# A hybrid encoder block on one core: the second half of the attention values and the first head pair as one operand of 512 columns, and the memory attention started behind later token blocks

## The chip, the core and the metric

The kernel runs on one core of a Trainium2 chip. A core has a matrix engine (TensorE, PE in the profile, with its weight loads as PEld), three elementwise engines (VectorE or DVE, ScalarE or ACT, GpSimd or POOL), a queue that issues transfers (SyncE or SP), an on-chip memory of 128 partitions, and a small accumulator memory of eight banks into which TensorE writes. The metric is the device time of one execution in microseconds; lower is better.

## The reference

One layer of a hybrid encoder on x (1024 tokens x 1024 channels) and a memory of 256 tokens. After an RMS norm, one input projection gives the inputs of three mixers and three sigmoid gates:

```python
h = _rmsnorm(x, norm_mix_g[l])
z = h @ w_in[l]
(hq, hf, hi, hg, fq, fk, fv, ff, mq, gate_logits) = split(z)
y_a = _hgrn2_mixer(hq, hf, hi, hg, ...)              # gated linear recurrence, 4 heads
y_b = _fox_mixer(fq, fk, fv, ff, fox_f_bias, ...)    # forgetting attention, 8 heads of 64
mem_kv = _rmsnorm(mem, norm_mem_g[l]) @ mem_kv_w[l]
y_c = _memory_mixer(mq, mem_kv, ...)                 # cross-attention into 256 memory tokens, 4 heads of 128
gates = sigmoid(gate_logits).reshape(B, T, 3, D_MODEL)
merged = gates[:, :, 0] * (y_a @ w_br_hgrn) + gates[:, :, 1] * (y_b @ w_br_fox) + gates[:, :, 2] * (y_c @ w_br_mem)
x = x + merged @ w_out
x = x + _conv_glu_ffn(_rmsnorm(x, norm_ffn_g[l]), ffn_w_up, ffn_conv_w, ffn_conv_b, ffn_w_down)
```

The forgetting attention needs, for each token, 512 values (fv), 8 forget logits (ff), and queries and keys of 8 heads (fq, fk). The memory attention normalizes its queries per head (a sum of squares over 128 channels), takes their products with 256 memory keys as logits, a softmax, and the product with the memory values.

## The kernel before

All matmuls are done on operands split into a rounded high part and a low remainder; a product is three matmuls (high x high, high x low, low x high) issued by `mm3` (lines 246 to 250). A split is a cast on ScalarE (line 254, the helper of all casts) and a subtraction on VectorE (line 262).

The program runs in stages. A dense stage computes most gates and the memory queries with a fast block scheme (`dense_unit`, products of the families T1 to T4, until about 267 us in the trace). Then comes the stage of this study:

- `token_major` (line 793) computes a projection with tokens on partitions. For each of 8 blocks of 128 tokens it issues 8 x 3 matmuls into one accumulator bank: the token block of `uh`/`ul` is the stationary operand, the split weights `wh`/`wl` are the moving one with `ncol` columns. An `evac` function then scales the bank by the tokens' norm and copies it out on ScalarE.
- `fox_values` (line 824) calls it twice: values 0 to 255 into `Vf` (256 columns, line 827), then values 256 to 511 with the 8 forget logits (264 columns, lines 827 and 829). After the second it turns the forget logits into cumulative log decays: absolute value, sigmoid and logarithm on ScalarE (lines 833 to 835), 8 transposes on TensorE (line 840), two scans on VectorE (line 841), and a store to DRAM.
- `fox_proj` (line 967) computes keys and queries of head pair 0 (256 columns) into `z` (line 973) and normalizes them in halves of four blocks (lines 979 to 982).
- `memory` (line 924) is the memory attention. `mem_prep(h)` loads the queries of a head (`mqf`, line 868), squares them (line 873), sums the squares with 8 one-column matmuls (line 876), and splits them into `mqh`/`mql`. `mem_parts` loads the memory's keys and values (`mkv`, line 858) and splits them. `mem_attn(h)` does, for each half of the tokens, logits (`mm3` into `lg`), maximum (897), exponential (901), normalization on GpSimd (905), transposes (912), a split, the product with the values (`po`), and a split and two stores of the result.

`weave` (line 98) traces these generators alternately: at each turn the one that is least far through its stated number of steps advances. The token work counts 25 steps, the memory 28, and both begin at share 0. The memory's instructions are traced under a priority 300 places ahead (`ahead`, line 236). The order on each engine within the stage is then made by a scheduler that puts together priority and expected readiness. The transfers are issued on SP in order.

Weights go through `weights` (line 276): a raw buffer (two in all, 512 KB a load), and a slot of a ring of four pairs `wh`/`wl` (`WIDE`), taken in turn. A piece of 1,024 columns holds four of the eight channel chunks of a 256-column projection, or two of a 512-column one.

After the weave come the weights of head pair 1 (`parts[-1]`, line 1332) and a stage whose order on every engine is written by a planner (`Plan`): first the tokens of pair 1 (line 1229, 256 columns), the transposes of `z` (line 1038), and then the forgetting attention.

Of the kernel before, what the change touches and what calls it, by code (L numbers as in the profile page):

```python
# [9 lines left out]
F32R = mybir.dt.float32r  # L10
AF = mybir.ActivationFunctionType
ALU = mybir.AluOpType
# [25 lines left out]

HGRN_STEPS, MEM_STEPS = 14, 7
AHEAD = 300  # L40
SLACK = 0.8
WIDE = 4
SEQ = ("w0 x0 s0 w1 x1 s1 w2 x2 s2 w3 x3 s3 w4 x4 s4 x5 s5 x6 s6 x7 s7 u0 u1 u2 u3 mn u4 u5 u6 u7 lk k0 k1 k2 k3 lx "
# [154 lines left out]
def tile_block(ctx: ExitStack, tc: tile.TileContext, xT, memT, x_rows, mem_rows, vec, fbias, mats, hmask, w_first, w_cm, w_late, w_fqk, w_fv,  # L198
# [47 lines left out]
    def mm3(ps, lh, ll, rh, rl, first, last, more=False):  # L246

        PE.matmul(ps, lh, rh, start=first, stop=False, skip_group_check=more)  # L248
        PE.matmul(ps, lh, rl, start=False, stop=False, skip_group_check=more)  # L249
        return PE.matmul(ps, ll, rh, start=False, stop=last, skip_group_check=more)  # L250
# [542 lines left out]
    def token_major(src, ncol, evac, lead=False):  # L793

        with tc.issue_after(late["load"].ins):
            per = 2 if ncol == HB else 4
            w = [weights(src[q], (per, ncol)) for q in range(KC // per)]
        if lead:
            yield
        for tb in range(8):  # L800
            ps = ps_proj()[:, :ncol]
            tsl = slice(tb * P, (tb + 1) * P)
            for k in range(KC):
                wh, wl = w[k // per]
                mm3(ps, uh[k][:, tsl], ul[k][:, tsl], wh[:, k % per, :], wl[:, k % per, :], k == 0, k == KC - 1)
            evac(tb, ps)
            yield


# [12 lines left out]
    negFd = tc.dram_tile([8, T], F32, name="negFd")  # L822

    def fox_values():
        for pc in range(2):
            def evac(tb, ps, pc=pc):
                S.activation(Vf[:, tb, pc * 256:(pc + 1) * 256], ps[:, :256], AF.Copy, scale=rt[:, tb:tb + 1])
                if pc:
                    V.scalar_tensor_tensor(out=ffx[:, tb, :], in0=ps[:, 256:264], scalar=rt[:, tb:tb + 1], in1=fbr,
                                           op0=ALU.mult, op1=ALU.add)  # L830
            yield from token_major(w_fv[pc], 264 if pc else 256, evac)

        S.activation(ffe, ffx, AF.Abs)
        S.activation(ffe, ffe, AF.Sigmoid)
        S.activation(ffe, ffe, AF.Ln)
# [27 lines left out]
    def mem_prep(h):  # L863
        mqh = pm.tile([P, T], F32R, tag="mqh", name=f"mqh_{h}", bufs=2)
        mql = pm.tile([P, T], F32R, tag="mql", name=f"mql_{h}", bufs=2)
        rq = pm.tile([P, 8], F32, tag="rq", name=f"rq_{h}", bufs=2)
        t = pm.tile([P, T], F32, tag="mqf", name=f"mqf_{h}", bufs=2)
        SP.dma_start(t, mqd[h])
        prs = ps_tr()
        for n in range(2):  # L870
            sl = slice(n * HB, (n + 1) * HB)
            sq = pm.tile([P, HB], F32, tag="msq2", name="msq2")
            S.activation(sq, t[:, sl], AF.Square)
            for b in range(4):
                tb = 4 * n + b
                PE.matmul(prs[:, tb:tb + 1], sq[:, b * P:(b + 1) * P], ones[:, 0:1], start=True, stop=True)
        split(S, mqh, mql, t)
        V.tensor_mul(rq, prs[:, :8], rt)
        V.tensor_mul(rq, rq, rt)
        rstd_small(rq, rq, P)  # L880
        V.tensor_mul(rq, rq, rt)
        mset[h] = (mqh, mql, rq)
        yield

    def mem_attn(h):
        mqh, mql, rq = mset[h]
        for n in range(2):
            pts = []
            for j in range(2):
                ps = ps_lg()  # L890
                pt = pm.tile([P, 2, NM], F32, tag="mpt", name="mpt", bufs=3)
                st = pm.tile([P, 8], F32, tag="mst", name="mst", bufs=3)
                tb = 4 * n + 2 * j
                for b in range(2):
                    tsl = slice((tb + b) * P, (tb + b + 1) * P)
                    mm3(ps[:, b * NM:(b + 1) * NM], mqh[:, tsl], mql[:, tsl], mkh[:, h, :], mkl[:, h, :], True, True)
                V.reduce_max(st[:, 0:2], ps.rearrange("p (b m) -> p b m", b=2), axis=AX.X)
                V.scalar_tensor_tensor(out=st[:, 2:4], in0=st[:, 0:2], scalar=-1.0, in1=rq[:, tb:tb + 2],
                                       op0=ALU.mult, op1=ALU.mult)
                for b in range(2):  # L900
                    S.activation(pt[:, b, :], ps[:, b * NM:(b + 1) * NM], AF.Exp, bias=st[:, 2 + b:3 + b],
                                 scale=rq[:, tb + b:tb + b + 1], accum_out=st[:, 4 + b:5 + b])
                V.reciprocal(st[:, 6:8], st[:, 4:6])
                for b in range(2):
                    G.tensor_scalar(pt[:, b, :], pt[:, b, :], st[:, 6 + b:7 + b], 0.0, ALU.mult, ALU.add)
                pts.append(pt)
                yield
            po = ps_po()
            for m in range(2):
                ptr = ps_tr()  # L910
                for b in range(4):
                    PE.transpose(ptr[:, b * P:(b + 1) * P], pts[b // 2][:, b % 2, m * P:(m + 1) * P], ident)
                ph = pm.tile([P, HB], F32R, tag="mph", name="mph", bufs=2)
                pl = pm.tile([P, HB], F32R, tag="mpl", name="mpl", bufs=2)
                split(S, ph, pl, ptr)
                hv = slice(h * P, (h + 1) * P)
                mm3(po, mvh[:, m, hv], mvl[:, m, hv], ph, pl, m == 0, m == 1)
            yt = [pm.tile([P, HB], F32R, tag=t, name=t, bufs=2) for t in ("ych", "ycl")]
            split(S, *yt, po)
            for t, d in zip(yt, ycd):  # L920
                SP.dma_start(d[:, h, n * HB:(n + 1) * HB], t.bitcast(F32))
            yield

    def memory():
        run_all(mem_prep(0))
        mem_parts()
        yield
        for h in range(4):
            if h < 3:
                run_all(mem_prep(h + 1))  # L930
            yield from mem_attn(h)
# [35 lines left out]
    def fox_proj():  # L967

        def evac(tb, ps):
            n, b = tb // 4, tb % 4  # L970
            if b == 0:
                fox_tile(0, n)
            S.activation(fox_z[0, n][:, b, :], ps, AF.Copy, scale=rt[:, tb:tb + 1])
            if b == 3:
                z = fox_z[0, n].rearrange("p b (h d) -> p (b h) d", d=64)
                r = cp.tile([P, 16], F32, tag="fr", name="fr", bufs=2)
                for i in range(2):
                    sq = gate_tile().rearrange("p (h d) -> p h d", d=64)
                    S.activation(sq, z[:, 8 * i:8 * i + 8, :], AF.Square)
                    V.reduce_sum(r[:, 8 * i:8 * i + 8], sq, axis=AX.X)  # L980
                rstd_small(r, r, 64)
                V.tensor_mul(z, z, r.unsqueeze(2).to_broadcast([P, 16, 64]))

        yield from token_major(w_fqk[0], 256, evac)

    qk, qk_ready, vh, vh_ready, nfs, nf_ready = {}, {}, {}, {}, {}, {}
    pt_ready, pt_free, rows_done, turn, kept = {}, {}, {-1: 0.0, -2: 0.0}, {}, {}
# [1108 lines left out]
def _layout(inp):  # L2096
# [6 lines left out]
    def kmaj(a):  # L2103

        return a.reshape(a.shape[0] // P, P, a.shape[1]).transpose(1, 0, 2)
# [52 lines left out]
    def pieces(a, cuts):  # L2158
        out = []
        for lo, hi_ in cuts:  # L2160
# [1 line left out]
            out.append(np.stack([p[:, 0:4].reshape(P, -1), p[:, 4:8].reshape(P, -1)]))  # L2162
        return out

    o["w_fqk"] = c(np.stack([pieces(np.concatenate([fk[:, p * P:(p + 1) * P], fq[:, p * P:(p + 1) * P]], axis=1),
                                    [(0, 256)])[0] for p in range(2)]))
    late = np.concatenate([m[:, p * P:(p + 1) * P] for p in (2, 3) for m in (fk, fq)], axis=1)
    o["w_late"] = c(np.stack([kmaj(m).reshape(P, 4, 2 * HB).transpose(1, 0, 2) for m in (late, hi)]))
    pv = pieces(np.concatenate([fv, ff], axis=1), [(0, 256), (256, 520)])
    o["w_fv0"], o["w_fv1"] = c(pv[0]), c(pv[1])  # L2170
# [32 lines left out]
```

## Time and profile before

| what | us |
| --- | --- |
| median of the three runs shown (1689.5 to 1692.33) | 1689.61 |
| the profiled execution's own time | 1688.31 |
| its span in the profile | 1686.5 |
| TensorE busy in the span | 1677.7 |
| VectorE, ScalarE, GpSimd busy | 1170.4, 808.5, 326.6 |
| the stage of this study, from and to | 258, 371 |

The span runs from the first to the last instruction; the execution's own time has the start and the end around it. A busy time of TensorE is made with modelled ends, so that the time of a matmul overlaps the next; what a matmul costs in a row of matmuls is the distance between two starts. Instructions stand under their source line, their output and their inputs (`pp<-wh,uh` is a matmul into a bank of the projections with moving `wh` and stationary `uh`). A time behind an arrow is idle time of the engine and what ended it.

### The profile page before, as it was taken

What the parts mean: (1) busy time and instruction counts of PE and PEld (TensorE: products, weight loads), DVE (VectorE), ACT (ScalarE), POOL (GpSimd) and SP (SyncE); (2) the same over time, 40 slices, a digit from 0 to 9 for tenths busy, and PEclk for the clock granted to TensorE, in tenths of its full rate; (3) what the DMA queues carried; (4) which work ended last, traced back from release to release, by engine and by line L of the source; (5) the groups of instructions that cost most, each with busy time, mean ns of one, the idle gap of its engine ahead of it and who ended that gap; (6) DMA issues with size and microseconds to landing.
All of it is one profiled execution on the core that took longest, in us unless ns stands there. A gap on an engine that the chain in (4) does not pass through costs nothing.

```text
span 1686.5 us, 23254 instructions
## 1 busy us (share of the span) xinstructions
PE 1677.7 (99%) x8409; PEld 1415.8 (84%) x8409; DVE 1170.4 (69%) x2118; ACT 808.5 (48%) x1459; POOL 326.6 (19%) x430
## 2 busy tenths in 40 slices
PE   9999999999999999999999999999999999999999
PEld 7888889998888888888888888888888888888887
DVE  6966554558688766766856745988788888775664
ACT  6734444656576556666521333634344444533432
POOL 0200001336464423433201000211111111100000
PEclk9999999999999999999999999999999999999999
DMA  9442324122142233100337641666454454494782
GB/s 376 171 145 105 118 77 157 71 100 69 57 133 87 75 101 101 51 20 19 107 106 257 207 151 58 189 180 182 132 144 131 122 166 132 176 352 154 239 283 88
DMA packets 87348, 235.50 MB, mean 140 GB/s; under 512 B 9904, under 2 KB 12600, under 8 KB 87104
## 3 DMA queue, kind: packets, MB, share of 16 engines
q1 hardware_dynamic: 68032, 166.83, 28.4%
q0 software_dynamic: 18624, 66.59, 13.9%
q8 instruction: 66, 1.08, 0.3%
q10 hardware_dynamic: 576, 0.59, 0.1%
q14 instruction: 50, 0.41, 0.1%
HBM read 184.91 MB, written 72.13 MB: 152 GB/s over the span
## 4 chain that ended last, share of the span: by engine, by line
PE 96%; DVE 2%; ACT 1%; DMA 1%; issue 0%; ACTq 0%; DVEq 0%
PE pp L250 17%; PE pp L249 17%; PE pp L248 17%; PE pp L1229 10%; PE lg L248 5%; PE lg L250 5%; PE lg L249 5%; PE tr L250 3%; PE tr L249 3%; PE tr L248 3%; PE tr L1147 2%; PE po L1172 1%; PE lg L1085 1%; PE lg L1086 1%; PE po L248 1%; PE po L249 1%
## 5 line engine op out<-in xcount | busy, mean ns | idle before, releaser
L254 ACT CAST wh<-s 128x512 fp32r<-128x512 f32 x122 | 73.3, 620 | 133.1 <-PE pp L249 73.3
L254 ACT CAST wh<-rw 128x512 fp32r<-128x512 f32 x96 | 58.5, 619 | 113.8 <-PE pp L249 69.7
L254 ACT CAST wh<-raw 128x512 fp32r<-128x512 f32 (+2 forms) x85 | 63.9, 756 | 96.0 <-PE pp L249 76.3
L254 ACT CAST dwh<-wr 128x1024 fp32r<-128x1024 f32 (+1 forms) x41 | 40.2, 980 | 114.1 <-PE tr L249 37.6
L250 PE MATMUL pp<-uh,wl 128*128 128x512 f32 x224 | 89.0, 397 | 0.0
L248 PE MATMUL pp<-uh,wh 128*128 128x512 f32 x224 | 88.8, 396 | 0.0
L249 PE MATMUL pp<-ul,wh 128*128 128x512 f32 x224 | 88.4, 395 | 0.0
L1161 DVE TENSOR_TENSOR pl<-tr,ph 128x512 fp32r<-128x512 f32 (+1 forms) x96 | 51.4, 551 | 30.7 <-ACT ph L254 30.3
L1120 ACT ACTIVATE pt<-pt,st 128x128 f32<-128x128 f32 (+3 forms) x64 | 49.6, 775 | 45.9 <-DVE st L1116 30.6
L1229 PE MATMUL pp<-wl,uh 128*128 128x512 f32 (+1 forms) x192 | 70.0, 365 | 0.0
L1229 PE MATMUL pp<-wh,uh 128*128 128x512 f32 (+1 forms) x192 | 69.5, 362 | 0.0
L1229 PE MATMUL pp<-wh,ul 128*128 128x512 f32 (+1 forms) x192 | 69.4, 362 | 0.0
L262 DVE TENSOR_TENSOR dwl<-wr,dwh 128x1024 fp32r<-128x1024 f32 (+1 forms) x41 | 46.3, 1130 | 30.5 <-ACT dwh L254 30.5
L254 ACT CAST ph<-tr 128x512 fp32r<-128x512 f32 (+1 forms) x96 | 44.2, 477 | 41.0 <-PE tr L1147 39.6
L1124 POOL TENSOR_SCALAR pt<-pt,st 128x128 f32<-128x128 f32 (+3 forms) x64 | 52.0, 815 | 60.1 <-DVE st L1122 58.4
L1828 POOL DMA_DIRECT2D rw<-in_w_up x42 | 23.2, 558 | 200.0 <-DVE wl L1718 190.1
L1718 DVE TENSOR_TENSOR wl<-rw,wh 128x512 fp32r<-128x512 f32 x69 | 46.6, 687 | 21.2 <-PE pp L250 17.9
L1718 DVE TENSOR_TENSOR wl<-s,wh 128x512 fp32r<-128x512 f32 x85 | 57.9, 683 | 0.0
L262 DVE TENSOR_TENSOR wl<-raw,wh 128x512 fp32r<-128x512 f32 (+2 forms) x54 | 52.1, 964 | 7.0 <-ACT wh L254 7.0
L248 PE MATMUL pp<-wh,uh 128*128 128x256 f32 (+1 forms) x192 | 55.2, 287 | 0.0
L250 PE MATMUL pp<-wh,ul 128*128 128x256 f32 (+1 forms) x192 | 55.0, 286 | 0.0
L249 PE MATMUL pp<-wl,uh 128*128 128x256 f32 (+1 forms) x192 | 54.4, 283 | 0.0
(520 smaller groups left out, 5602.2 us busy)
## 6 DMA issues: line engine op xcount, KB each, us to landing
rw<-in_w_up POOLq DMA_DIRECT2D x42, 512.0 KB, 4.8
sd<-in_w_dn POOLq DMA_DIRECT2D x30, 512.0 KB, 6.0
br<-yd SPq DMA_DIRECT2D x30, 512.0 KB, 5.6
gd<-gt SPq DMA_DIRECT2D x48, 256.0 KB, 2.0
gt<-gd SPq DMA_DIRECT2D x48, 256.0 KB, 2.8
yd<-fc SPq DMA_DIRECT2D x44, 256.0 KB, 2.8
wr<-sd SPq DMA_DIRECT2D x20, 512.0 KB, 4.9
raw<-in_w_cm SPq DMA_DIRECT2D x18, 512.0 KB, 3.5
```

The costliest lines, as they stand in the source:

```text
L248: PE.matmul(ps, lh, rh, start=first, stop=False, skip_group_check=more)
L249: PE.matmul(ps, lh, rl, start=False, stop=False, skip_group_check=more)
L250: return PE.matmul(ps, ll, rh, start=False, stop=last, skip_group_check=more)
L254: return S.copy(out, in_)
L262: return (sub or V).tensor_sub(l, src, h.bitcast(F32))
L1120: S.activation(pt, pt, AF.Exp, bias=st[:, 2:3], accum_out=st[:, 3:4])
L1124: G.tensor_scalar(pt, pt, st[:, 3:4], 0.0, ALU.mult, ALU.add)
L1147: PE.transpose(ptr[:, j * P:(j + 1) * P], pts[j][:, sb * P:(sb + 1) * P], ident)
L1161: V.tensor_sub(pl[:, c], ptr[:, c], ph[:, c].bitcast(F32))
L1229: PE.matmul(o, a, b, start=q == i == 0, stop=q == KC - 1 and i == 2)
L1718: late["split"] = V.tensor_sub(l, src, h.bitcast(F32))
L1828: late["raw"] = (SP if begun else G).dma_start(raw[:, 2 * i:2 * i + 2, :], src[:, 2 * i:2 * i + 2, :])
```

## The change

The second half of the values and head pair 0 become one operand of 512 columns (`wide`, `w_fv[1]`), computed in one `token_major` pass by `fox_proj`, which evacuates each block twice: 256 columns to `z`, 256 to `Vf`. The first pass now holds the first half of the values with the forget logits (264 columns), so the decays are computed between the two passes. The 512-column weights have four pieces of two chunks; the third one is split into a pair of tiles of its own (`xwh`, `xwl`, from the stage's pool), and the fourth takes the next slot of the ring. The token work counts 17 steps in the weave, and the memory begins at share 0.2 and waits until five token blocks have been traced. For head 0, the matmuls of the norm sums and of the logits are ordered behind the last token matmul traced before them.

```diff
+MEM_START = 0.2
...
         with tc.issue_after(late["load"].ins):
             per = 2 if ncol == HB else 4
-            w = [weights(src[q], (per, ncol)) for q in range(KC // per)]
+            own = [pm.tile([P, 4 * 264], F32R, tag=t, name=t) for t in ("xwh", "xwl")] if ncol == HB else None
+            w = [weights(src[q], (per, ncol), hl=own if q == 2 else None) for q in range(KC // per)]
...
-                mm3(ps, uh[k][:, tsl], ul[k][:, tsl], wh[:, k % per, :], wl[:, k % per, :], k == 0, k == KC - 1)
+                late["tokens"] = mm3(ps, uh[k][:, tsl], ul[k][:, tsl], wh[:, k % per, :], wl[:, k % per, :], k == 0, k == KC - 1)
             evac(tb, ps)
+            late["blocks"] = late.get("blocks", 0) + 1
             yield
...
     def fox_values():
-        for pc in range(2):
-            def evac(tb, ps, pc=pc):
-                S.activation(Vf[:, tb, pc * 256:(pc + 1) * 256], ps[:, :256], AF.Copy, scale=rt[:, tb:tb + 1])
-                if pc:
-                    V.scalar_tensor_tensor(out=ffx[:, tb, :], in0=ps[:, 256:264], scalar=rt[:, tb:tb + 1], in1=fbr,
-                                           op0=ALU.mult, op1=ALU.add)
-            yield from token_major(w_fv[pc], 264 if pc else 256, evac)
+        def evac(tb, ps):
+            S.activation(Vf[:, tb, :256], ps[:, :256], AF.Copy, scale=rt[:, tb:tb + 1])
+            V.scalar_tensor_tensor(out=ffx[:, tb, :], in0=ps[:, 256:264], scalar=rt[:, tb:tb + 1], in1=fbr,
+                                   op0=ALU.mult, op1=ALU.add)
+        yield from token_major(w_fv[0], 264, evac)
...
-                PE.matmul(prs[:, tb:tb + 1], sq[:, b * P:(b + 1) * P], ones[:, 0:1], start=True, stop=True)
+                with tc.issue_after(late["tokens"].ins) if h == 0 else nullcontext():
+                    PE.matmul(prs[:, tb:tb + 1], sq[:, b * P:(b + 1) * P], ones[:, 0:1], start=True, stop=True)
...
-                    mm3(ps[:, b * NM:(b + 1) * NM], mqh[:, tsl], mql[:, tsl], mkh[:, h, :], mkl[:, h, :], True, True)
+                    with tc.issue_after(late["tokens"].ins) if h == 0 else nullcontext():
+                        mm3(ps[:, b * NM:(b + 1) * NM], mqh[:, tsl], mql[:, tsl], mkh[:, h, :], mkl[:, h, :], True, True)
...
         run_all(mem_prep(0))
         mem_parts()
         yield
+        while late["blocks"] < 5:
+            yield
...
-            S.activation(fox_z[0, n][:, b, :], ps, AF.Copy, scale=rt[:, tb:tb + 1])
+            S.activation(fox_z[0, n][:, b, :], ps[:, 256:], AF.Copy, scale=rt[:, tb:tb + 1])
+            S.activation(Vf[:, tb, 256:], ps[:, :256], AF.Copy, scale=rt[:, tb:tb + 1])
...
-        yield from token_major(w_fqk[0], 256, evac)
+        yield from token_major(w_fv[1], HB, evac)
...
-    weave((chain(fox_values(), fox_proj()), 25), (ahead(memory(), AHEAD), 4 * MEM_STEPS))
-    parts[-1] = [(weights(w_fqk[1][q], (4, 256)), q, 0.0) for q in range(2)]
+    weave((chain(fox_values(), fox_proj()), 17), (ahead(memory(), AHEAD), 4 * MEM_STEPS, MEM_START))
+    parts[-1] = [(weights(w_fqk[q], (4, 256)), q, 0.0) for q in range(2)]
```

The rest of the diff lays the weights out on the host to match: `w_fv0` has the first 256 value columns and the 8 forget logits, `w_fv1` the other 256 value columns and the 256 columns of pair 0, `w_fqk` pair 1 alone.

More of the change, by code (lines that the diff above doesn't have):

```diff
@@ L2163, in pieces @@
         return out
-    o["w_fqk"] = c(np.stack([pieces(np.concatenate([fk[:, p * P:(p + 1) * P], fq[:, p * P:(p + 1) * P]], axis=1),
-                                    [(0, 256)])[0] for p in range(2)]))
+    pair = [np.concatenate([fk[:, p * P:(p + 1) * P], fq[:, p * P:(p + 1) * P]], axis=1) for p in range(2)]
+    o["w_fqk"] = c(pieces(pair[1], [(0, 256)])[0])
+    wide = np.concatenate([fv[:, 256:], pair[0]], axis=1)
     late = np.concatenate([m[:, p * P:(p + 1) * P] for p in (2, 3) for m in (fk, fq)], axis=1)
     o["w_late"] = c(np.stack([kmaj(m).reshape(P, 4, 2 * HB).transpose(1, 0, 2) for m in (late, hi)]))
-    pv = pieces(np.concatenate([fv, ff], axis=1), [(0, 256), (256, 520)])
-    o["w_fv0"], o["w_fv1"] = c(pv[0]), c(pv[1])
+    o["w_fv0"] = c(pieces(np.concatenate([fv[:, :256], ff], axis=1), [(0, 264)])[0])
+    o["w_fv1"] = c(kmaj(wide).reshape(P, 4, 2 * HB).transpose(1, 0, 2))
     kv = f["mem_kv_w"][0]
```

## The prediction

> **What bounds the kernel now.** I read the page's busy shares first, then the chain that ended last, then the stretches of the stage that the change touches, and last the order of single instructions in it.
>
> ```profile
> span 1686.5 us, 23254 instructions
> PE 1677.7 (99%) x8409; PEld 1415.8 (84%) x8409; DVE 1170.4 (69%) x2118; ACT 808.5 (48%) x1459; POOL 326.6 (19%) x430
> PE 96%; DVE 2%; ACT 1%; DMA 1%; issue 0%; ACTq 0%; DVEq 0%
> ```
>
> TensorE is busy for 99% of the span, and 96% of the chain that ended last is TensorE. The stage in question (values, head pair 0, and the memory attention woven between them) runs from 258 to 371 us. The stretches view has, after the length, the busy time of each engine, the clock, and the DMA share and rate:
>
> ```profile
> core 0: us, PE busy (x) PEld busy (x) DVE busy (x) ACT busy (x) POOL busy (x), PEclk, DMA share, GB/s
> 265.00:275.00 10.00, 10.00 (x77) 9.60 (x76) 1.95 (x2) 3.29 (x6) 0.00 (x0) 1.00 0.78 268
> 285.00:295.00 10.00, 10.00 (x88) 10.00 (x87) 6.35 (x16) 8.48 (x18) 3.93 (x6) 1.00 0.37 125
> 258.00:371.00 113.00, 113.00 (x886) 109.33 (x885) 57.97 (x123) 64.35 (x143) 27.57 (x39) 1.00 0.26 90
> ```
>
> TensorE fills 113.00 of 113.00 us at full granted clock (1.00); ScalarE has 64 and VectorE 58. Nothing makes TensorE wait, so this stage is worth exactly the sum of its matmuls, and a change gains only by making that sum smaller. It can lose by making TensorE wait at all, since there is no gap to absorb it.
>
> The length of a matmul is modelled with its pipeline drain; what it costs is the step to the next one. The chain in order of time gives that directly, as start, time on the chain, line and count:
>
> ```profile
> 369.69 0.23 PE po L250
> 370.75 0.96 PE pp L1229 x8
> 372.58 9.48 PE pp L1229 x79
> 382.06 0.44 PE tr L1038 x4
> 655.11 10.98 PE pp L1229 x48
> ```
>
> The 79 matmuls at 372.58 have 256 columns: 9.48 / 79 = 0.1200 us. The 48 at 655.11 have 512: 10.98 / 48 = 0.2288 us, less than twice 0.1200.
>
> **The change, part by part.** The groups of the stage by shape give the counts (the means include the drain):
>
> ```profile
> L248 PE MATMUL pp<-wh,uh 128*128 128x256 f32 x128 | 36.7, 286 | 0.0
> L248 PE MATMUL pp<-wh,uh 128*128 128x264 f32 x64 | 18.5, 289 | 0.0
> L248 PE MATMUL pp<-T3h,wh 128*128 128x512 f32 x4 | 1.6, 392 | 0.0
> ```
>
> *The merged operand.* A product of two split operands is three matmuls (lines 248 to 250); the rows are those of line 248, and the other two lines have the same counts. The 3 x 128 = 384 matmuls of 256 columns are two passes, the first half of the values and pair 0. The 264-column pass keeps its 3 x 64 matmuls (it now takes the first half of the values with the forget logits, and comes first). The second half of the values and pair 0 become one pass of 8 blocks x 8 x 3 = 192 matmuls of 512 columns. Removed: 384 x 0.1200 = 46.08 us. Added: 192 x 0.2288 = 43.93 us. Difference: -2.15 us. With the fastest 512 steps there are (stationary token blocks, as here; first and last of 26 steps),
>
> ```profile
> 655.72 0.40 PE L1229 MATMUL pp<-uh,wh 128*128 128x512 f32 x1
> 661.63 0.39 PE L1229 MATMUL pp<-uh,wl 128*128 128x512 f32 x1
> ```
>
> it is (661.63 - 655.72) / 26 = 0.2273 each, 43.64 in all, -2.44 us. So this part is worth 2.15 to 2.44 us, and I take 2.15 since the block steps will be broken by attention pieces. The Trainium skill ("TensorE: Matmul & The Clock Gate", Back-to-back issue gap) puts a warm matmul at N/2.4 plus about 2.5 ns, that is 109.2 and 215.8 ns. By that the merge would save only 384 x 0.1092 - 192 x 0.2158 = 0.5 us and the sum below would be -0.1; the steps measured here carry more than 10 ns above N/2.4, so the measurement decides against it.
>
> *Evacuations.* Today:
>
> ```profile
> L827 ACT ACTIVATE Vf<-pp,rt 128x256 f32<-128x256 f32 x16 | 7.7, 478 | 7.9 <-PE pp L250 7.8
> L973 ACT ACTIVATE z<-pp,rt 128x256 f32<-128x256 f32 x8 | 3.8, 475 | 7.0 <-PE pp L250 7.0
> ```
>
> That is 16 of Vf and 8 of z. After: 8 of Vf in the first pass and 8 of Vf plus 8 of z in the second. Count and size are the same, on an engine with 49 of 113 us free: nothing. After the last block one more evacuation (about 0.5 us) stands ahead of the norm of z. The transposes at 382.06 that need that norm have a margin:
>
> ```profile
> 375.87 1.64 DVE L982 TENSOR_TENSOR z<-z,fr 128x1024 f32<-128x1024 f32 x1 [3.02 <-POOL fr L267]
> ```
>
> z is done at 377.5 and wanted at 382.06, so 4.5 us cover it.
>
> *Weights.* Eight pieces of 1,024 columns (two of them 1,056) stay eight: 2 + 4 + 2 in place of 2 + 2 + 2 + 2. But the merged pass holds four at once. Its third piece gets its own two tiles; its fourth (q = 3) must take the slot that the first pass frees with its last block. Where the same slot is refilled today:
>
> ```profile
> 291.13 1.06 ACT L254 CAST wh<-raw 128x1024 fp32r<-128x1024 f32 x1
> 292.22 1.23 DVE L262 TENSOR_TENSOR wl<-raw,wh 128x1024 fp32r<-128x1024 f32 x1 [0.65 <-ACT wh L254]
> 337.35 1.06 ACT L254 CAST wh<-raw 128x1024 fp32r<-128x1024 f32 x1
> ```
>
> Cast to end of subtraction is 292.22 + 1.23 - 291.13 = 2.32 us. TensorE reaches q = 3 after 12 more matmuls of the first pass (1.44 us) and 18 of the second (4.12 us): 5.56 us of cover, 3.2 us to spare. So nothing, as long as the cast isn't queued for over 3.2 us. Likewise the second piece of pair 1 now takes a slot that comes free 18 matmuls (4.1 us) before the end of the stage, in place of some 33 us before (337.35). Pair 1 wants it 12 matmuls in (1.4 us), again 5.5 against 2.32: nothing.
>
> *The pins and the later start.* Memory traces its first steps after four and five token blocks; a norm sum of head 0 may not pass block 4 and its first logits not block 5. What stands there now:
>
> ```profile
> 267.12 0.28 PE L250 MATMUL pp<-wh,ul 128*128 128x256 f32 x1
> 277.07 0.28 PE L249 MATMUL pp<-wl,uh 128*128 128x256 f32 x1
> 277.19 0.95 PE L876 MATMUL tr<-ones,msq 128*128 128x1 f32 x8
> 279.16 0.40 PE L248 MATMUL lg<-mkh,mqh 128*128 128x256 f32 x2
> 280.84 0.28 PE L249 MATMUL lg<-mkl,mqh 128*128 128x256 f32 x1
> ```
>
> From 258 to 277.19 are 19.2 us, of which the last two dense products (T3 above and T4, 3 x 4 matmuls each) take 24 x 0.2288 = 5.5. The other 13.7 are about 114 token matmuls at 0.1200, or 4.7 blocks of 24, ahead of the first norm sum; with those from there to 279.16 it is 5.1 blocks ahead of the first logits. From 267.12 to 277.07 they stand without a break. The pins ask for 96 and 120: both hold already. What sets the start is the arrival of head 0's operands, whose loads are issued only at 269.88 and 270.42 (rows below), and these steps keep their lead in priority, so tracing them four blocks later moves none of their loads. So the pins cost nothing and gain nothing.
>
> *Loads.* One weight load moves. Of the issues on SP, the first below fills the raw buffer that the merged pass will use for its third piece; the row after it has size and time to landing:
>
> ```profile
> 264.43 0.34 SPq L273 DMA_DIRECT2D raw<-in_w_fqk  x1
> raw<-in_w_fqk SPq DMA_DIRECT2D x4, 512.0 KB, 3.5
> 269.88 0.45 SPq L868 DMA_DIRECT2D mqf<-mqd  x1
> 270.42 0.38 SPq L858 DMA_DIRECT2D mkv<-kvd  x1
> 276.32 1.05 POOL L258 TENSOR_SCALAR mkh<-mkv 128x1024 fp32r<-128x1024 f32 x1 [67.57 <-DMA mkv<-kvd]
> 278.37 1.21 DVE L262 TENSOR_TENSOR mkl<-mkv,mkh 128x1024 fp32r<-128x1024 f32 x1
> ```
>
> Today that buffer stays full until a slot is free (the cast at 291.13). With tiles of its own the third piece is split at once, and the buffer is free near 264.43 + 3.5 + 2.32 = 270.3 (an estimate). The next load, for pair 1, then joins head 0's queries and keys, issued at 269.88 and 270.42. At 268 GB/s (the stretch 265:275) 512 KB take 2.0 us. The low keys are ready at 279.58 and used at 280.84: 1.26 us of margin. Bounds: 0 if the load comes behind, 2.0 - 1.3 = 0.7 us if it all goes ahead. I take 0.4.
>
> *Decays.* The forget-logit chain (three activations, 8 transposes at L840, two scans) moves from 340 to about 294, its cost on TensorE unchanged.
>
> Sum: -2.15 + 0.4 = -1.75 us. Against the profiled execution's own 1688.3 us that is 1686.6; that run stands 1.3 us under the median of the three shown (1689.6), so for the median I say **1687.8**.
>
> **The rivals.**
>
> *A: ScalarE gets crowded where the passes meet, and TensorE waits (slower).* The place is 285 to 305. ScalarE is 85% busy in 285:295 already, with head 0's exponentials and splits, and the decays' chain now lands there, with its table loads:
>
> ```profile
> 340.86 1.28 ACT L834 ACT_TABLE_LOAD   x1
> 342.43 1.28 ACT L835 ACT_TABLE_LOAD   x1
> 351.39 1.28 ACT L901 ACT_TABLE_LOAD   x1
> ```
>
> Three loads and three activations of 0.26 are 4.6 us; exponentials falling between the sigmoid and the logarithm add two loads, 2.6 us. 8.5 + 4.6 to 7.2 us of work for 10 us is a backlog of 3 to 6 us. It decides from where the cast of q = 3 is over 3.2 us late. The attention pieces that TensorE's fixed order expects come late too: at each such wait up to those 3 to 6 us, and at two of them, the block's and the attention's, 6 to 9. Time: 1687.8 + 4 to 9 = 1692 to 1697. For it: the last of the three loads belongs to the attention's own exponentials, which already stand behind the chain today, and the chain is moved to a fuller place. Against it: TensorE has token blocks there to run in the meantime, and it never stood during the same pause today (113.00 of 113.00). The Trainium skill ("ScalarE activation tables: per-element evaluation and per-set limits", What a function is on this engine) says that two functions of different sets stand one table load of 1283 ns apart; the three rows above agree.
>
> *B: the merge is paid back (no change).* The attention ends at 369.69 + 0.23, under 1 us before the next pair's matmuls at 370.75. If its own latency sets its end, 2.15 us less token work only uncovers its tail, and the stage ends where it did: 1689.6. Against it: 88 matmuls of pair 1 need only weights and can fill in.
>
> *C: faster than the matmul count allows.* The new order would also have to take away waits after 371. The whole page has few: the three small ones before 1,100 us in the view of waits are
>
> ```profile
> PE lg L1523 <- DVE X L1501: 0.7, 1, 0.7
> PE po L1172 <- DVE pl L1161: 0.5, 1, 0.5
> PE lg L1085 <- DVE st L1099: 0.4, 1, 0.4
> ```
>
> 1.6 us in all, which with 2.44 from the merge makes 1689.6 - 4.0 = 1685.6.
>
> **How the numbers follow.** The forecast (1686.9 to 1688.6) gets 0.45, A 0.33, B 0.09, C 0.13. No change means within 0.2% (3.4 us, about what a measurement of this kernel can tell from no change); the forecast and B lie inside it: 0.54. A is slower, 0.33; C is faster, 0.13. The range reaches from just under C's time, 1685.5, to 1696, which leaves out the last part of A.
>
> **What would show it.** Right: one group of 192 matmuls of 512 columns on token blocks with steps of 0.227 to 0.232, no 256-column ones but pair 1's and the logits'; TensorE full through the stage; next pair's first matmul near 369 us. Wrong: an idle stretch of TensorE near 297 that ends with a split of weights or near 281 with the low keys (A and the load); more than three table loads in the stage (A); TensorE idle in the last 5 us of the stage (B).

## The result, and the profile after

The changed kernel takes 1697.6 us (median of 6 runs, 1694.5 to 1699.58) where the kernel before takes 1689.47 (6 runs beside them): ratio 1.0048, 95% interval 1.0035 to 1.0060, or 8.1 us more. The prediction was 1687.8 us, with 1685.5 to 1696.0 as its range: the change is slower, and by more than the range allowed. The profiled execution, 1694.5 us, is the fastest of the six, and its span is 6.2 us longer than that of before. The page's lines on the whole:

```profile
span 1692.7 us, 22860 instructions
PE 1678.3 (99%) x8217; PEld 1407.4 (83%) x8217; DVE 1171.7 (69%) x2118; ACT 807.5 (48%) x1459; POOL 325.2 (19%) x430
PE 95%; DVE 2%; ACT 1%; DMA 1%; issue 0%; POOL 0%; SPq 0%; ACTq 0%; DVEq 0%
```

There are 192 matmuls fewer, and TensorE is still 99% busy: neither number says where 6 us went. The stage does. The groups of its matmuls by shape (busy us, mean ns of one, idle time before them and what ended it):

```profile
L249 PE MATMUL pp<-wh,uh 128*128 128x264 f32 x64 | 19.4, 303 | 4.3 <-DVE ffx L830 4.3
L249 PE MATMUL pp<-wh,uh 128*128 128x512 f32 x48 | 19.1, 399 | 0.0
L249 PE MATMUL pp<-xwh,uh 128*128 128x512 f32 x16 | 6.4, 402 | 0.0
```

And two single ones near its end, five steps apart:

```profile
369.95 0.40 PE L249 MATMUL pp<-wh,uh 128*128 128x512 f32 x1
371.11 0.39 PE L251 MATMUL pp<-wh,ul 128*128 128x512 f32 x1
```

The merge is there as predicted: 3 x (48 + 16) = 192 matmuls of 512 columns, at (371.11 - 369.95) / 5 = 0.232 us in this stretch. But in the last column of the first group stands an idle time that before did not have. The view of TensorE's waits, for the stage and the 27 us behind it (us in total, times, longest):

```profile
PE pp L249 <- DVE ffx L830: 4.3, 1, 4.3
PE lg L1091 <- DVE st L1105: 1.2, 1, 1.2
PE po L249 <- DVE ycl L263: 0.8, 1, 0.8
```

In the same stretch of the kernel before the view lists none; the wait of line 1085 (now 1091) that the prediction quoted, 0.4 us, lies at 504 us. The first wait in single rows, in order of time: SP, TensorE, VectorE, TensorE.

```profile
270.63 0.38 SPq L821 DMA_DIRECT2D fbr<-in_fbias  x1
272.01 0.28 PE L251 MATMUL pp<-wh,ul 128*128 128x264 f32 x1
276.23 0.36 DVE L830 SCALAR_TENSOR_TENSOR ffx<-pp,rt,fbr 128x8 f32<-128x8 f32 x2 [4.14 <-DMA fbr<-in_fbias]
276.61 0.56 PE L249 MATMUL pp<-wh,uh 128*128 128x264 f32 x1 [4.32 <-DVE ffx L830]
276.96 0.42 PE L250 MATMUL pp<-wl,uh 128*128 128x264 f32 x1
281.36 0.34 PE L249 MATMUL pp<-wh,uh 128*128 128x264 f32 x1
```

The pass with the forget logits now comes first. Its evacuation adds the forget biases `fbr` (line 830), a load of 4 KB that SP issues at 270.63, behind the loads of head 0. Three banks fill, the first is not released, and the matmul of the fourth block waits until the biases are there. Before, the same evacuation began 28 us after the load:

```profile
L829 DVE SCALAR_TENSOR_TENSOR ffx<-pp,rt,fbr x8: 214/226/227, 299.0 to 339.8; 128x8 f32<-128x8 f32 x8
```

The wait has a second part. The stretches view (length, PE busy, granted clock, DMA share, GB/s) of the changed kernel:

```profile
271.00:276.60 5.60, 1.29 (x11) 0.83 0.91 359
276.70:281.30 4.60, 4.60 (x21) 0.50 0.13 39
281.50:286.00 4.50, 4.50 (x41) 1.00 0.47 141
```

Behind the stop the clock is half: (281.36 - 276.96) / 20 = 0.220 us a matmul where 0.121 is the rule. In the two profiled executions the sum up to head pair 1 is: merge -2.15 (192 x 0.2288 against 384 x 0.1200), stop 276.61 - 272.01 - 0.12 = +4.48, half clock 4.75 - 21 x 0.121 = +2.21, the wait near 375 +0.84. Together +5.4. From the first token matmul (258.16 before, 257.96 after) to the 13th matmul of pair 1 (372.90 and 378.70) the changed kernel takes 6.0 us longer. Steps of 0.232 in place of 0.2288, if all 192 have them, would be the other 0.6 (an estimate). Behind that the wait of line 1091 adds 1.2, and about as much comes back near 510 us, where matmuls of the same line stand late in the kernel before and not in the changed one; so the spans differ by 6.2. The other 1.9 us of the medians lie in runs of which there is no profile. The granted clock of four of the five is 0.998 over the whole span, as in the profiled one, so they show no longer half clock; what it is stays open.

### The profile page after: what moved, and what is told of

It reads as the page before. It is cut to its first block, busy times and chain, and to the rows that moved or that the text cites. A ratio compares the mean times of both kernels' runs of the same rounds, so it can differ in the third digit from the quotient of the medians.

```text
span 1692.7 us, 22860 instructions
## 1 busy us (share of the span) xinstructions
PE 1678.3 (99%) x8217; PEld 1407.4 (83%) x8217; DVE 1171.7 (69%) x2118; ACT 807.5 (48%) x1459; POOL 325.2 (19%) x430
## 4 chain that ended last, share of the span: by engine, by line
PE 95%; DVE 2%; ACT 1%; DMA 1%; issue 0%; POOL 0%; SPq 0%; ACTq 0%; DVEq 0%
PE pp L250 17%; PE pp L249 17%; PE pp L251 17%; PE pp L1235 9%; PE lg L249 5%; PE lg L250 5%; PE lg L251 5%; PE tr L250 3%; PE tr L249 3%; PE tr L251 3%; PE tr L1153 2%; PE po L1178 1%; PE lg L1091 1%; PE po L249 1%; PE po L1177 1%; PE po L250 1%
## 5 line engine op out<-in xcount | busy, mean ns | idle before, releaser
L250 PE MATMUL pp<-yl,wh 128*128 128x512 f32 x128 | 50.1, 392 | 0.0
L249 PE MATMUL pp<-yh,wh 128*128 128x512 f32 x128 | 50.1, 397 | 0.0
L249 PE MATMUL pp<-T2h,wh 128*128 128x512 f32 x128 | 50.0, 391 | 0.0
```

## The experiments

Two theories stood at first. *Bias*: the late biases, with the half clock behind them, are the whole loss, and without them the merge's 2.15 us appear. *Tail*: something else in the new order costs too, and shows once the wait is gone. Later the second was divided: the decays' chain in the middle (D), the attention's later start, or the merge itself (M). Times are medians beside runs of the kernel before on the same chip; differences are ratios times 1689 us.

**The biases loaded at the start** (changed kernel otherwise).

```diff
-    top.tile([P, 56], F32, tag="fill", name="fill_top")
+    top.tile([P, 48], F32, tag="fill", name="fill_top"); fbr = top.tile([P, 8], F32, tag="fb", name="fb")
...
-    SP.dma_start(ident, mats[:, 0:P])
+    SP.dma_start(ident, mats[:, 0:P]); SP.dma_start(fbr, fbias)
...
-    fbr = pm.tile([P, 8], F32, tag="fbr", name="fbr")
-    SP.dma_start(fbr, fbias)
```

> The changed kernel, but the 8 forget biases are loaded once at the start of the kernel into a tile that is kept, not at 270.6 us. Theory L (late bias: the first pass now ends in evacuations that need the biases, they land at 276.2, three accumulator banks fill up and TensorE stands 4.6 us and then runs some 24 matmuls at half clock): the wait and the slow matmuls are both gone, and what is left is the merge's gain: 1686 to 1689 us. Rival M (the loss comes from the attention's later start, its pins and the weight hand-over): the bias is one late thing among several, the attention's operands come as late as before and TensorE waits for them instead: 1693 to 1697 us.

Measured 1695.56 us, ratio 1.0036 (1.0023 to 1.0049). The wait near 272 is gone, and only about 2 us come back. TensorE now comes to the end of the token blocks at 363.4, and then has little but the attention to work on. Its waits in the same stretch:

```profile
PE tr L915 <- POOL mpt L908: 3.4, 1, 3.4
PE po L250 <- DVE mpl L263: 1.1, 1, 1.1
PE lg L1091 <- DVE st L1105: 0.7, 1, 0.7
PE po L249 <- ACT mph L255: 0.6, 1, 0.6
```

What POOL does at that time, and then the stretch behind it (the clock is third from the end):

```profile
368.24 2.90 POOL L268 TENSOR_TENSOR fr<-fr,mhalf 128x16 f32<-128x16 f32 x1 [5.27 <-DVE fr L267]
371.12 1.99 POOL L908 TENSOR_SCALAR mpt<-mpt,mst 128x256 f32<-128x256 f32 x2
```

```profile
372.80:377.00 4.20, 3.56 (x11) 2.25 (x12) 1.29 (x2) 1.07 (x2) 1.52 (x3) 0.64 0.00 0
```

The attention's last part has nothing left to hide behind: 30 of its matmuls stand behind the last token matmul, and three of its steps are waited for. For the longest, the normalization on POOL, the norm of `z` stands ahead on that engine. And the clock falls again. Its last store goes at 378.6 in both kernels: the wait for the biases had only covered this one. So the bias theory holds for the wait and falls for the whole.

**The two value passes swapped, nothing merged** (kernel before otherwise): `for pc in (1, 0)` in `fox_values`.

> The kernel before with nothing changed but the order of its two value passes: the one with the forget logits goes first. No merge, no pins, no later start. Theory L: the same wait appears, with the same half-clock stretch: 6 to 8 us over the kernel before, 1695.5 to 1697.5. Rival M: no loss, 1689 to 1690.5.

Measured 1695.14 us, ratio 1.0036 (1.0022 to 1.0049), a little under the range of theory L. The order of the passes alone brings back the same stop, under another line's name, since the first norm sum stands there in the order. Single rows of TensorE and VectorE, and the stretch behind them:

```profile
277.48 1.86 PE L876 MATMUL tr<-ones,msq 128*128 128x1 f32 x8 [3.90 <-ACT msq L873]
278.24 0.36 DVE L829 SCALAR_TENSOR_TENSOR ffx<-pp,rt,fbr 128x8 f32<-128x8 f32 x2 [7.75 <-DMA fbr<-in_fbias]
```

```profile
277.50:281.00 3.50, 3.50 (x16) 3.50 (x17) 2.76 (x5) 1.49 (x2) 1.04 (x1) 0.50 0.04 8
```

**The biases loaded at the start in the kernel before.** The edit is the first one's.

> The kernel before with the biases loaded at the start. Its order on TensorE is the same. Both theories: within 1 us of the kernel before (1688.5 to 1690.5), since nothing there waits for the biases; it shows what the early load itself costs.

Measured 1689.28 us, ratio 0.9999 (0.9990 to 1.0009): where the biases are not late, loading them early is worth nothing, so the runs with early biases can be compared with before.

**The wait filled** (changed kernel, biases late): 18 matmuls of 512 columns that nobody reads stand between blocks three and four of the first pass, so that TensorE never stops there. The token matmuls behind them are ordered after them.

```diff
+            if ncol == 264 and tb == 3:
+                dummy = ps_tr()
+                with tc.issue_after(late["tokens"].ins):
+                    for _ in range(18):
+                        late["fill"] = PE.matmul(dummy, uh[0][:, :P], uh[0][:, :HB], start=True, stop=True)
...
+                with tc.issue_after(late["fill"].ins) if "fill" in late else nullcontext():
```

> The changed kernel with 18 matmuls of 512 columns, whose results nobody reads, put on TensorE between the third and the fourth token block of the first pass (18 x 0.227 = 4.1 us), so that TensorE is busy while the bias lands; the rest of the order is the same. If the half clock comes from TensorE standing still, it is gone: 1697.6 less 2.4 (25 matmuls of 0.22 in place of 0.12) to less 5 (if the runs that took 1697 had a longer stretch of it): 1692.5 to 1695.2. If the clock fell for another reason, the time is that of the changed kernel, 1697 to 1698, and if the bias isn't the cause, 1701 (4.1 us more).

Measured 1694.49 us, ratio 1.0033 (1.0021 to 1.0046): 2.5 us less than the changed kernel (3.1 by the medians), with the same work and idle work in place of the wait. That is the half clock's share, beside 2.21 from the rows above. The two profiled executions agree up to pair 1, where this one is 2.4 us ahead (second table below), though not in all: 1694.31 against 1694.5, since other waits take the lead back later, 0.6 us at line 1241 (1235 in the changed kernel) among them. Its clock in the same stretch (columns as before, the clock third from the end):

```profile
276.70:281.30 4.60, 4.60 (x40) 4.60 (x41) 2.98 (x4) 0.92 (x2) 0.42 (x1) 1.00 0.15 42
```

**Swapped passes with early biases, nothing merged, nothing pinned.** Both edits together on the kernel before.

> The kernel before, with the two value passes swapped (forget logits first, so the decays' chain lands in the middle of the attention) and the biases loaded at the start; nothing is merged and nothing is pinned. Theory M (the merge itself is what leaves the attention's tail without cover): as the kernel before, 1687 to 1691, the attention's last product before the last token block ends. Theory D (the decays' chain in the middle delays the attention): the attention ends late here too, TensorE waits in the last 8 us of the stage, 1693 to 1696.

Measured 1690.37 us, ratio 1.0009 (0.9999 to 1.0018). The decays' chain lies at 301 to 305 here, and the attention ends earlier than before (last store 368.6 against 370.6). Theory D falls as the reason for a late attention where nothing is merged and the attention does not start later. What the chain does cost here is one wait, behind the third table load of the chain:

```profile
304.31 1.28 ACT L901 ACT_TABLE_LOAD   x1 [0.43 <-PE tr L912]
306.86 0.38 PE L248 MATMUL lg<-mkh,mqh 128*128 128x256 f32 x1 [1.01 <-ACT mpt L901]
```

**The decays' chain behind the merged pass** (changed kernel with early biases).

```diff
-    weave((chain(fox_values(), fox_proj()), 17), (ahead(memory(), AHEAD), 4 * MEM_STEPS, MEM_START))
+    weave((chain(fox_values(), fox_proj(), fox_decays()), 17), (ahead(memory(), AHEAD), 4 * MEM_STEPS, MEM_START))
...
+    def fox_decays():
```

> The kernel after, biases loaded at the start, and the decays' chain moved behind the merged pass; merge, pins and later start stay. Theory D: the attention ends 5 to 6 us earlier, no wait over 1 us in the last 10 us of the stage, 1687 to 1689. Theory M: the written order still has 20 attention matmuls behind the last token matmul, TensorE waits there for 5 us and more, 1693 to 1696.

Measured 1692.05 us, ratio 1.0017 (1.0008 to 1.0026): between the two expectations. The attention ends some 5 us earlier, as D said, but 20 of its matmuls are still behind the tokens, and the decays' scans now hold up the transposes of `z`:

```profile
PE tr L1044 <- DVE negF L842: 2.0, 2, 1.7
PE po L249 <- DVE ycl L263: 0.8, 1, 0.8
```

Beside the run with the early biases alone this is still 3.2 us less (1.0017 against 1.0036). So with the merge and the later start in place the chain in the middle does cost; the run before this one, without both, shows only the wait of 1.0 us.

**Without the later start and the pins** (early biases): merge and new order of the passes alone.

```diff
-MEM_START = 0.2
+MEM_START = 0.0
...
-                with tc.issue_after(late["tokens"].ins) if h == 0 else nullcontext():
+                with nullcontext():
...
-        while late["blocks"] < 5:
-            yield
```

> The kernel after, biases loaded at the start, without the pins and without the attention's later start: the merge and the new order of the passes alone. If the pins or the later start delay the attention: attention's end near 370, 1687 to 1689. If they change nothing, as the prediction said: tail as in the run with the early biases, waits of 5 us and more behind the last token block, 1693 to 1696.

Measured 1690.12 us, ratio 1.0008 (0.9999 to 1.0017), 4.7 us less than with both, and between the two expectations. The pins and the later start were not run apart, but the pins can have next to no part in it: written out without the pins alone, the order of VectorE, ScalarE, GpSimd and SP is the same, and on TensorE one matmul moves. So it is the later start. It does not delay the first logits (279.15 us with it, 279.16 in the kernel before); by the order of the instructions it moves the later steps of the attention back against the token blocks.

The merge is in here without late biases and without late start, and the medians still show no gain: 1690.1 against 1690.4 for the swap alone. Three waits of half a microsecond and more are left:

```profile
PE pp L1235 <- ACT z L1255: 1.5, 1, 1.5
PE lg L1091 <- DVE st L1105: 1.3, 1, 1.3
PE po L249 <- ACT mph L255: 0.6, 1, 0.6
```

The first comes 12 us after the attention's last matmul. SP issues in order, and the next stage's weights stand behind the attention's last stores; ScalarE waits for them, and an evacuation of pair 1 waits behind ScalarE. SP, ScalarE and TensorE:

```profile
374.27 0.32 SPq L924 DMA_DIRECT2D ychd<-ych  x1
376.00 0.32 SPq L924 DMA_DIRECT2D ycld<-ycl  x1
378.61 12.55 SPq L1213 DMA_DIRECT2D raw<-in_w_late  x3
385.89 0.62 ACT L255 CAST wh<-raw 128x512 fp32r<-128x512 f32 x1 [8.45 <-DMA raw<-in_w_late]
386.93 0.38 PE L1235 MATMUL pp<-wh,uh 128*128 128x256 f32 x1 [1.46 <-ACT z L1255]
```

In the kernel before the first of these stores goes at 370.57 and the load at 373.32.

**The merged pass first**, early biases, no pins and no later start, the attention traced a little earlier.

```diff
-    weave((chain(fox_values(), fox_proj()), 17), (ahead(memory(), AHEAD), 4 * MEM_STEPS, MEM_START))
+    weave((chain(fox_proj(), fox_values()), 12), (ahead(memory(), AHEAD), 4 * MEM_STEPS, MEM_START))
```

> Merge, early biases, no pins, the merged pass before the pass with the forget logits, and the attention's steps traced a little earlier against the token blocks (12 in place of 17 in the weave): in the order written out no attention matmul is left behind the last token block. Theory M (what costs is the attention's tail without cover): the merge's 2.15 us come back, 1686.5 to 1688.5, no TensorE wait over 1 us between 258 and 371. If blocks of 512 columns slow the attention whatever the order says: TensorE waits in the tail, 1690 to 1695.

Measured 1698.73 us, ratio 1.0052 (1.0040 to 1.0065): a miss. No attention matmul is left behind the tokens, but the decays' chain now comes last, and nothing hides it. Two of its table loads on ScalarE, and on TensorE the transposes of the decays that the order puts ahead of those of `z`:

```profile
374.61 1.28 ACT L835 ACT_TABLE_LOAD   x1
376.18 1.28 ACT L836 ACT_TABLE_LOAD   x1
378.13 1.14 PE L841 MATMUL tr<-ident,ffe 128*8 128x128 f32 x8 [4.24 <-DVE ffe L837]
```

One latency had been exchanged for another, with a granted clock of 0.59 behind it (378.2 to 382.2). The run doesn't decide for or against theory M.

**Late biases without the later start** (the edit of the run without the later start, on the changed kernel as it is).

> The kernel after without the attention's later start (and without the pins); the biases still come late, as in the kernel after. If the three costs add up (the late biases with the half clock behind them, the later start, the rest): the wait for the biases stays at 4 us and the slow stretch behind it, the tail as in the run without pins; 1690.1 + 4.3 + 2.5 = 1697. If the two hide each other in part, because the wait gives the attention's operands time to arrive: 1693 to 1695.

Measured 1693.53 us, ratio 1.0024 (1.0015 to 1.0034): 2.7 us above the run with early biases, less than the full sum. The stop is shorter here and no wait stands in the tail; yet the half clock follows, from 274.99 to 281.8 us (rows in the last section):

```profile
274.99 1.86 PE L878 MATMUL tr<-ones,msq 128*128 128x1 f32 x8 [2.70 <-ACT msq L874]
```

**Each merged block as two runs of 256 columns** (early biases, no pins, no later start): everything of the merge but the long matmul.

```diff
-            for k in range(KC):
-                wh, wl = w[k // per]
-                late["tokens"] = mm3(ps, uh[k][:, tsl], ul[k][:, tsl], wh[:, k % per, :], wl[:, k % per, :], k == 0, k == KC - 1)
+            for c in ((slice(0, 256), slice(256, HB)) if ncol == HB else (slice(0, ncol),)):
+                for k in range(KC):
+                    wh, wl = w[k // per]
+                    late["tokens"] = mm3(ps[:, c], uh[k][:, tsl], ul[k][:, tsl], wh[:, k % per, c], wl[:, k % per, c], k == 0, k == KC - 1)
```

> The run without pins and later start, biases early, and each merged block computed as two runs of 256 columns one after the other into the two halves of its bank; loads, evacuations and passes stay those of the merge. If TensorE's own work sets the time: slower than the run without pins by 384 x 0.1200 - 192 x 0.2288 = 2.15 us, 1692.3. If the attention's tail sets it and the long matmuls hold the attention up (in the order written out no attention matmul is left behind the last token matmul here, and 74 token matmuls, 8.9 us, are behind the last of the attention): TensorE without a wait in the tail, attention's last store near 368, time 1689 to 1690.5, the same or less.

Measured 1690.5 us, ratio 1.0007 (0.9998 to 1.0016): 2.15 us more matmul work, and the same time. The last store goes almost 10 us earlier than with the long matmuls, the next weights 11 us earlier, and one wait of TensorE is left, behind the decays' chain. The view of waits, and SP's rows:

```profile
PE lg L249 <- ACT mpt L905: 0.8, 1, 0.8
```

```profile
364.49 0.32 SPq L925 DMA_DIRECT2D ychd<-ych  x1
367.20 26.86 SPq L1214 DMA_DIRECT2D raw<-in_w_late  x4
```

Each of the two ratios is uncertain by 0.0009, 1.5 us, so the times alone would hardly tell 2.15 us from nothing; the traces say the same (second table below). Theory M stands: the waits that the long matmuls bring (1.5 + 1.3 + 0.6 + 0.2 = 3.6 us against 0.8) are worth about what they save. In the trace from 294 to 363 us, the stretches of six and more token matmuls between two pieces of the attention's stage are 1.8 us long in the median with halves and 3.5 with the long matmuls (18 and 12 stretches). That the attention is slower because of these stretches fits, but was not tried apart from the rest.

**The attention traced earlier** (early biases, no pins, no later start; 12 in place of 17 in the weave, the passes in the order of the change).

> The run without pins and later start, biases early, with the attention's steps traced earlier against the token blocks (12 in place of 17 in the weave); the written order has 15 in place of 20 attention matmuls behind the last token matmul. If the written order of the attention sets the tail: part of the 4 us of waits behind 370 goes, 1688 to 1689.5. If not: 1690 as there.

Measured 1690.72 us, ratio 1.0010 (1.0001 to 1.0019): no gain. The wait near 386 is gone, and others of 0.9, 0.7 and 0.6 us stand in its place.

The last matmul of the token blocks and of the attention, by the traces:

| kernel | last token matmul, us | last attention matmul, us | attention matmuls behind the tokens | ratio |
| --- | --- | --- | --- | --- |
| before | 370.5 | 369.5 | 0 | 1 |
| changed | 371.1 | 377.6 | 20 | 1.0048 |
| changed, early biases | 363.4 | 377.6 | 30 | 1.0036 |
| the same, decays last | 365.6 | 372.0 | 20 | 1.0017 |
| no later start, early biases | 366.3 | 373.2 | 20 | 1.0008 |
| the same, in halves | 372.4 | 363.4 | 0 | 1.0007 |
| swap alone, early biases | 373.0 | 367.5 | 0 | 1.0009 |

None of these kernels is faster than the one before.

The positions in this table hold an offset that the change did not make: the first token matmul of the stage stands anywhere from 257.96 to 259.89 us in the profiled executions. The second table therefore counts from it, to the 13th matmul of pair 1 and to one matmul of the next stage, the same in all kernels, at 519.80 us in the kernel before:

| kernel | first token matmul, us | to the 13th of pair 1, us | to the matmul near 520, us |
| --- | --- | --- | --- |
| before | 258.16 | 114.74 | 261.64 |
| before, early biases | 259.89 | 114.74 | 262.25 |
| swap alone, early biases | 259.67 | 115.80 | 261.46 |
| changed | 257.96 | 120.74 | 267.80 |
| changed, wait filled | 258.14 | 118.32 | 266.20 |
| changed, early biases | 258.28 | 120.41 | 266.42 |
| no later start, early biases | 259.87 | 114.50 | 262.87 |
| the same, in halves | 259.30 | 115.56 | 262.25 |
| no later start, traced earlier | 259.69 | 115.09 | 261.15 |

Up to pair 1 the merge does gain, 1.3 us on the swap alone and 1.1 on the halves. Near 520 us the gain is gone. These are single executions, and the first two rows, whose kernels differ in nothing that is waited for, are 0.6 us apart in the last column.

## Why the prediction was wrong

Put on one after the other, the parts come to the whole (ratios times 1689): swapped passes with early biases +1.5, the merge on top -0.2, the late biases on top +2.7, the later start on top +4.1, together +8.1. Each single step is uncertain by 2 us and more, so the first two are not told from nothing by these times. The shares depend on the order: with the later start in place, the late biases cost only 2.0, because one wait covers the other, and without the merge they cost 4.6.

- *The merged operand*: right as a term of TensorE's work (192 matmuls, 0.232 us in the rows above; up to pair 1 it gives 1.3 us of the 2.15), wrong as a gain. The prediction's premise, that "this stage is worth exactly the sum of its matmuls", holds only while the attention ends inside the token work. Before it did by about 1 us (369.5 against 370.5). The figure of the Trainium skill ("TensorE: Matmul & The Clock Gate", Back-to-back issue gap) that the prediction set against its own steps is, by that section's words, the gap of an isolated matmul and not of a row with a weight load before each, as here; nothing in the sum hung on it.
- *Decays*: the step that failed first. "The forget-logit chain ... moves from 340 to about 294, its cost on TensorE unchanged" looked at the chain and not at what the pass ahead of it reads. The biases' load, issued at 270.99, is the issue next behind the last one quoted. Its first use moves from 299 to about 269 (269.4 with the biases early), and it lands at 276; so the fourth block waits 4.3 us. Neither this wait nor the half clock behind it was priced, and no rival had them.
- *The pins and the later start*: right for the pins; wrong for the start. "These steps keep their lead in priority, so tracing them four blocks later moves none of their loads" is true of head 0 and its first logits, and says nothing of the seven half heads behind them. Cost: 4.1 to 4.7 us, in part through the decays' chain (moved behind the tokens, it gives about 3.2 us back).
- *Rival B* (the merge paid back, 0.09): this fits what the runs with early biases and without the later start show, at 1690.1 us where it said 1689.6. The reason against it failed: "88 matmuls of pair 1 need only weights and can fill in". The order written out puts 8 of them ahead of the transposes of `z` (lines 1229 and 1038, now 1235 and 1044), and in the changed kernel those stand among the attention's last matmuls, at 376.89 and 377.79. The trace of before had that too: 8 matmuls at 370.75 stand apart from the 79 at 372.58 in the chain quoted, and the argument used the larger number.
- *Rival A* (ScalarE crowded, 0.33): it gave the right side, and its range reached nearly to the result, for another reason. Its mechanism is real where the passes are swapped (1.0 and 0.8 us near 305, behind the chain's table load), but a quarter or less of the 4 to 9 us it asked; in the changed kernel no wait stands there.
- *Rival C* (waits behind 371 us go away): waits came there instead, 1.2 us at line 1091 in the changed kernel.
- *Evacuations, weights*: nothing, as said. No wait on a weights piece and none on the norm of `z` appears in the changed kernel. *Loads*: the load for pair 1 does join head 0's; no wait for the low keys appears, so the 0.4 us were not needed.
- *What would show it*: "TensorE idle in the last 5 us of the stage (B)" is the sign that came (0.84 us near 375, and 5 us of waits in the run with early biases). The idle stretch near 281 that was listed for the low keys came at 272, for the biases.

## What to carry to other kernels

When a pass moves ahead, follow every operand of its evacuation back to the issue of its load, however small it is: 4 KB cost a stop of 4.3 us and a half clock behind it. Before counting a gain on a busy TensorE, ask which latency chain ends beside the work that is taken away, and with how much to spare; here it was 1 us, and the 2.15 us saved were paid back there and, through the in-order queue of transfers, once more in the next stage. And long matmuls leave fewer breaks for a chain that is woven between them, which fits the run in halves but was not tried by itself.

## What was not expected of the hardware

- A load of 4 KB took 5.5 us from issue to landing, behind two of 512 KB issued within the microsecond before it. The row of the transfers between 268 and 278 us in the changed kernel, with size and time to landing:

```profile
fbr<-in_fbias SPq DMA_DIRECT2D x1, 4.0 KB, 5.5
```

- A stop of a few microseconds halves the clock for 3.4 or 6.8 us. Stretches cut where the clock changes, for the changed kernel, the one without the later start (late biases) and the one with early biases (length, PE busy, granted clock, DMA share, GB/s):

```profile
271.25:274.65 3.40, 1.04 (x9) 1.00 0.99 395
274.66:281.48 6.82, 4.87 (x22) 0.50 0.35 129
271.58:274.98 3.40, 0.71 (x6) 1.00 1.01 377
275.00:281.80 6.80, 6.80 (x31) 0.50 0.53 167
370.55:373.95 3.40, 0.88 (x4) 1.00 0.40 154
373.97:377.36 3.39, 3.13 (x9) 0.50 0.00 0
```

  The half clock begins where a stretch of 3.4 us ends in which TensorE was busy for 0.7 to 1.0 us (1.3 in the swap with late biases, 0.8 with the merged pass first, both with 6.8 us of half clock behind). With 1.74 us of work in such a stretch (decays last, 373.2 to 376.6) it stayed at 1.00. So a stop of 2.7 us cost as long a half clock as one of 4.3. The Trainium skill ("TensorE: Matmul & The Clock Gate", What's actually happening) says that the gate goes to half after one idle window of about 3.4 us and back after a busy one, the window running freely. The half clock and its lengths agree; by these rows a window counts as idle with up to 1.3 us of work in it.
